# Modulation from free tiles, the sink as a score column, and a wider output projection in a two-layer hybrid attention kernel

## Chip, cores and metric

The kernel runs on one core of a Trainium2 chip. Times are device microseconds of one launch. The engines are named as in the profile: PE is TensorE, PEld its weight load, DVE VectorE, ACT ScalarE, POOL GpSimd, SP SyncE, which here only issues DMAs.

## What is computed

Two layers over 512 latent tokens and 256 context tokens of 1024 channels. Each layer normalises its tokens and modulates them by vectors from the conditioning (`w_mod`, 1024 x 3072 for each layer, gives shift, scale and gate), projects them by `w_in`, and feeds three attention branches: latent attention (MLA, 8 heads), differential attention (8 heads) and windowed attention with a sink logit for each of its 16 heads. Each branch's output is gated, projected by `w_branch`, weighted by a sigmoid gate and summed, and the sum goes through `w_out`:

```python
h_lat = rms_norm(x, norm_g) * (1.0 + scale) + shift
qc_l, kvc_l, kr_l, dq_l, dk_l, dv_l, sq_l, sk_l, sv_l, z_l, gm_l = split_cols(h_lat @ w_in)
...
p = jax.nn.softmax(jnp.concatenate([sk] + [s.astype(jnp.float32) for s in parts], axis=-1), axis=-1)
...
return (terms[0] + terms[1] + terms[2]) @ w_out
...
x = x + gate * merge_branches((ya_l, yb_l, yc_l), z_l, gm_l, w_branch, w_out)
```

`sk` is the sink: one logit for each head that takes part in the softmax and has no value behind it. The context tokens go the same way in the first layer; in the second only their keys and values are needed. The result is the latent stream after a final RMS norm with the weights `final_norm`.

## The kernel before, in words

All of it is one program whose order on every engine is written out beforehand by a planner. `Plan` keeps a simulated time and the time at which each engine is free (`P.on`, `P.pe`, `P.tick`, with costs such as `mm_cost` or the 550 ns of a modulation piece). Chains of instructions are Python generators that yield the time at which they are ready; `flush` emits the chain with the lowest rank first (`RANK`, line 42), and among equals the one that is ready first. Two streams feed PE: `stream_a` has the attention units (scores, transposes, values), `stream_b` the entries of a list (`plan_b`): the projections in the order of `SEQ`, then, for each branch, gates z and g and branch outputs b in the order of `BR`. An entry of `stream_b` starts when enough tiles are free (`need`, and `keep` more for the others), and the next one waits for it. What is emitted is fixed then; on the chip each engine works through its own list in order.

**Tiles and queues.** SBUF holds 46 large tiles of 128 x 768 (`slot`, `room`, `free`), nine of 128 x 512 (`pt`, taken by `tmps`), eight of 128 x 256 (`yo`). Weights come through `weight_stream`: a ring of two tiles `ws` (`NWS`) takes 512 KB at a time; each is split by ACT and DVE into a high and a low fp32r part in a ring of six tiles `wh` (`NWH`), since every product of the kernel is made of three fp32r passes (line 444 emits them). All DMAs are issued by SP (line 341).

**Modulation.** `mod_mm` (line 579) is a product with a stationary operand of 32 columns, written to the partitions 32g to 32g + 31 of a PSUM bank, g being the row block modulo 4. For the first layer's shift and scale this is done in the head (`mod_now`, eight products in a row). The other eight blocks of 512 columns (two for the gate of the first layer, six for the second) are done by `mod_entry`: four entries for each block, each with one tile `ws` of the weight ring and two products of 512 columns. They are put between the z, g and b entries of the first layer. `mod_fin` adds the four partial sums.

**Windowed attention.** `soft_sink` (line 849) works on a row of 128 queries of one head: a DVE instruction adds the mask and takes the maximum with the sink (858), another changes its sign (861), ACT takes the exponential of the sink alone and then of the row with its sum, DVE adds the two sums, takes the reciprocal (865), and `normalise` scales the row. There are 96 such rows in the first layer and 64 in the second.

**Output projection.** `out_entry` goes through four chunks of 256 columns, each for all tokens: for each half of the 1024 inputs and each token four steps of three passes into one PSUM bank. Each token's chain multiplies by the gate, adds the residual, squares with a sum, and after the last chunk normalises (`norm_rows` in the first layer; `rstd`, a scaling with `final_norm` and two stores in the second).

**Head.** `begin` loads modulation weights, x and the context tokens; `setup`, `setup1` and `setup2` load the small vectors (c, biases, norms, the lambda vectors of the differential attention, the sinks). `setup2`'s chain multiplies the lambda vectors on DVE.

## Time and profile before

| | us |
|---|---|
| median of 3 runs | 2752.4 |
| lowest and highest | 2744.74, 2753.49 |
| the profiled execution: its own time | 2746.83 |
| its span | 2745.0 |
| PE busy | 2657.7 |
| DVE, ACT, POOL busy | 1655.3, 1380.5, 127.8 |
| mean granted clock of PE | 0.988 |

The span is what the profile shows of one execution; the own time is a little longer. Times of rows are counted from the span's start. "busy" is the time in which an engine had an instruction at work; matmuls overlap, so the mean of one is longer than the step from one to the next, and that step is read from rows of equal matmuls in the timeline. What stands in brackets is idle time before an instruction and what ended it.

### The profile page before, as it was taken

To read this page: it belongs to the slowest core of one execution; us is meant where nothing else is said; L and a number is where in the kernel's file an instruction comes from. 1 tells how busy PE (TensorE), PEld (TensorE's weight loads), DVE (VectorE), ACT (ScalarE), POOL (GpSimd) and SP (SyncE) were. 2 spreads that over 40 slices of the span, in tenths; PEclk is the share of its full clock that TensorE was granted. 3 is DMA by queue.
4 is the path that set the end of the run, shared out by engine and by line. 5 is a ranking of instruction groups with operands and counts; after the bars stand their busy time and mean duration, and the time that the engine had idled before them with its cause. 6 is when DMAs were issued, how large, how long until landed. Compare 5 with 4: busy or idle time off the path is not lost.

```text
span 2745.0 us, 42932 instructions
## 1 busy us (share of the span) xinstructions
PE 2657.7 (97%) x16711; PEld 2308.7 (84%) x16711; DVE 1655.3 (60%) x3350; ACT 1380.5 (50%) x2860; POOL 127.8 (5%) x198
## 2 busy tenths in 40 slices
PE   7999999999999999999999999999999999999998
PEld 4888898888888878878888988898888789888888
DVE  4678778666676652133333578888767677634435
ACT  4667777555556442121222357877546555523332
POOL 0000000111100000000000000000011100000000
PEclk8999999999999999999999999999999999999999
DMA  6132211111122353353332443322112223443433
GB/s 228 45 92 83 73 42 46 49 51 48 44 68 87 107 187 105 93 175 93 91 86 62 139 125 92 105 57 67 40 48 55 58 68 102 127 136 110 123 101 130
DMA packets 328348, 249.58 MB, mean 91 GB/s; under 512 B 24548, under 2 KB 288320, under 8 KB 328144
## 3 DMA queue, kind: packets, MB, share of 16 engines
q1 hardware_dynamic: 328144, 246.83, 30.9%
q8 instruction: 131, 2.15, 0.3%
q14 instruction: 73, 0.60, 0.1%
HBM read 211.37 MB, written 35.41 MB: 90 GB/s over the span
## 4 chain that ended last, share of the span: by engine, by line
PE 78%; DVE 9%; ACT 7%; issue 3%; DMA 2%; POOL 1%; SPq 0%; DVEq 0%; ACTq 0%; POOLq 0%
PE wd L444 37%; PE bk L444 35%; PE bk L913 4%; ACT pt L309 3%; ACT s L309 3%; DVE pt L323 2%; DVE s L323 2%; PE bk L579 1%; DVE wh L323 1%; DVE s L858 1%; DVE s L330 1%; ACT wh L309 1%; DMA ws<-in_w_in_dram 1%; DVE ti L825 0%; POOL pt L325 0%
## 5 line engine op out<-in xcount | busy, mean ns | idle before, releaser
L444 PE MATMUL wd<-s,wh 128*128 128x512 f32 (+1 forms) x4392 | 855.5, 355 | 6.7 <-ACT wh L309 3.5
L444 PEld LDWEIGHTS wd<-s,wh 128*128 128x128 f32 x4392 | 725.7, 189 | 145.0 <-ACT s L309 12.9
L444 PE MATMUL bk<-s,wh 128*128 128x512 f32 (+1 forms) x3666 | 771.7, 356 | 18.4 <-DVE s L323 6.9
L444 PEld LDWEIGHTS bk<-s,wh 128*128 128x128 f32 x3666 | 582.5, 190 | 106.6 <-DVE s L323 9.8
L323 DVE TENSOR_TENSOR wh<-ws,wh 128x1024 fp32r<-128x1024 f32 (+4 forms) x294 | 325.1, 1112 | 343.1 <-ACT wh L309 341.4
L309 ACT ACTIVATE wh<-ws 128x1024 fp32r<-128x1024 f32 (+4 forms) x294 | 282.5, 967 | 297.1 <-PE wd L444 148.5
L309 ACT ACTIVATE pt<-bk 128x512 fp32r<-128x512 f32 (+3 forms) x604 | 341.4, 584 | 167.9 <-PE bk L913 102.8
L444 PE MATMUL bk<-wh,s 128*128 128x256 f32 x2688 | 352.9, 286 | 3.8 <-DVE wh L323 2.0
L444 PEld LDWEIGHTS bk<-wh,s 128*128 128x128 f32 x2688 | 333.3, 193 | 9.7 <-issue 3.2
L323 DVE TENSOR_TENSOR pt<-bk,pt 128x512 fp32r<-128x512 f32 (+3 forms) x400 | 257.6, 664 | 77.7 <-ACT pt L309 66.4
L444 PE MATMUL bk<-pt,s 128*128 128x256 f32 x1888 | 277.2, 288 | 13.3 <-DVE pt L323 10.2
L444 PEld LDWEIGHTS bk<-pt,s 128*128 128x128 f32 x1888 | 252.2, 191 | 38.8 <-DVE pt L323 16.7
L444 PE MATMUL wd<-s,s 128*128 128x256 f32 (+5 forms) x1872 | 275.9, 333 | 5.9 <-ACT s L309 5.5
L309 ACT ACTIVATE s<-wd,ti 128x768 f32<-128x768 f32 (+1 forms) x240 | 195.5, 818 | 140.8 <-DVE ti L825 78.5
L444 PEld LDWEIGHTS wd<-s,s 64*128 64x128 f32 (+2 forms) x1872 | 214.3, 191 | 36.7 <-ACT s L309 9.9
L913 PE MATMUL bk<-ident,s 128*128 128x128 f32 x1472 | 208.5, 275 | 9.8 <-DVE pt L323 2.4
L913 PEld LDWEIGHTS bk<-ident,s 128*128 128x128 f32 x1472 | 170.3, 142 | 35.9 <-ACT s L309 5.5
L309 ACT ACTIVATE s<-s,ti 128x512 f32<-128x512 f32 (+3 forms) x249 | 174.1, 708 | 15.0 <-DVE ti L865 8.1
L309 ACT ACTIVATE s<-bk 128x256 fp32r<-128x256 f32 (+5 forms) x291 | 113.6, 424 | 87.0 <-PE bk L444 85.0
L330 DVE SCALAR_TENSOR_TENSOR s<-s,wd 128x768 f32<-128x768 f32 (+1 forms) x58 | 47.6, 820 | 180.8 <-PE wd L444 108.1
L309 ACT ACTIVATE s<-wd 128x768 f32<-128x768 f32 (+1 forms) x58 | 40.9, 705 | 218.8 <-PE wd L444 218.8
L825 DVE TENSOR_REDUCE ti<-wd 128x1 f32<-128x768 f32 (+1 forms) x160 | 128.7, 843 | 18.2 <-PE wd L444 17.9
(98 smaller groups left out, 1734.6 us busy)
## 6 DMA issues: line engine op xcount, KB each, us to landing
ws<-in_w_in_dram SPq DMA_DIRECT2D x180, 512.0 KB
ws<-in_w_branch_dram SPq DMA_DIRECT2D x48, 512.0 KB
ws<-in_w_mod_dram SPq DMA_DIRECT2D x32, 512.0 KB
ws<-in_w_out_dram SPq DMA_DIRECT2D x24, 512.0 KB
y<-yo SPq DMA_DIRECT2D x80, 128.0 KB
s<-y SPq DMA_DIRECT2D x24, 384.0 KB
s<-s SPq DMA_DIRECT2D x22, 384.0 KB
s<-in_w_mod_dram SPq DMA_DIRECT2D x32, 256.0 KB
```

Source lines behind the costliest of these rows:

```text
L309: lambda: nc.scalar.activation(out=out, in_=in_, func=func, scale=scale, **kw))
L323: t = yield from dve(ready, lambda: nc.vector.tensor_tensor(out=out, in0=a, in1=b, op=op), n)
L330: t = yield from dve(ready, lambda: nc.vector.scalar_tensor_tensor(out=out, in0=a, scalar=s, in1=b, op0=op0, op1=op1), fsz(out), ptr=ptr)
L444: nc.tensor.matmul(o, lhsT=l, rhs=r, start=first, stop=last)
L579: nc.tensor.matmul(pm[32 * g:32 * g + 32, :], lhsT=sil[:, kt], rhs=wv, start=kt < 4, stop=kt >= 4)
L825: t = yield from dve(t, lambda: nc.vector.tensor_reduce(out=nmx, in_=p[:, lo:hi], axis=AX.X, op=ALU.max, negate=True), n)
L858: t = yield from dve(t, lambda: nc.vector.tensor_tensor_reduce(out=pt_[:, 0:n], in0=p[:, lo:hi], in1=mk, scale=1.0, scalar=sk, op0=ALU.add ...
L913: nc.tensor.transpose(out=pp[:, j * 256 + ri2 * 128:j * 256 + ri2 * 128 + 128], in_=row["P"][:, c:c + 128], identity=ident)
```

## The change

Six things. (1) A modulation piece takes 256 columns and all eight row blocks instead of 512 columns and two; its weights go in three DMAs to three free large tiles instead of the weight ring, and its products are a piece of their own for the planner (`P.pe`). (2) The scores and the mask of the windowed attention change their sign, the sink is copied by POOL as one more column behind the row, and one exponential with scale -1 covers row and sink with one sum. (3) The output projection takes 512 columns at a time, except that the second half of the latent tokens' columns is done in two steps of 256, the last one token by token; `final_norm` is multiplied in before the square sums are complete, and the last scaling is shared by ACT and DVE; the residuals are loaded before the gates. (4) The small vectors of `setup` and `setup1` are issued by ACT, those of `setup2` by POOL. (5) The values of the windowed attention are computed for the latent tokens first. (6) The weight splitter's rank goes from 2 to 1. The diff, cut to its core:

```diff
-RANK = (0, 1, 3, 0, 2)
+RANK = (0, 1, 3, 0, 1)
...
-    below = np.where(j >= i, 0.0, -1e30)
-    above = np.where(j <= i, 0.0, -1e30)
+    below = np.where(j >= i, 0.0, 1e30)
+    above = np.where(j <= i, 0.0, 1e30)
...
-    def dma(out, in_):
-        nc.sync.dma_start(out=out, in_=in_)
+    def dma(out, in_, eng=nc.sync):
+        eng.dma_start(out=out, in_=in_)
...
-        n, t = rows_of(sc, (c_in[0], c_ctx))
+        n, t = rows_of(sc, (c_in[0], c_ctx), nc.scalar)
...
-        dma(selt, sel)
+        dma(selt, sel, nc.scalar)
         st = slot()
-        n, t = rows_of(st, (b_mod[0], norm_g[0]))
+        n, t = rows_of(st, (b_mod[0], norm_g[0]), nc.scalar)
...
-        n, t = rows_of(st, (q_norm[0], kv_norm[0], subln[0], b_mod[1], norm_g[1], q_norm[1], kv_norm[1], subln[1]))
+        n, t = rows_of(st, (q_norm[0], kv_norm[0], subln[0], b_mod[1], norm_g[1], q_norm[1], kv_norm[1], subln[1]), nc.gpsimd)
         tv = 0.0
         for i, a in enumerate((lq1, lk1, lq2, lk2)):
-            tv = max(tv, dma(v[:, i * 128:(i + 1) * 128], a.rearrange("l d -> (l d)").partition_broadcast(128)))
-        dma(sinkt, sink.rearrange("l h -> (l h)").partition_broadcast(128))
+            tv = max(tv, dma(v[:, i * 128:(i + 1) * 128], a.rearrange("l d -> (l d)").partition_broadcast(128), nc.gpsimd))
+        ts = dma(sinkt, sink.rearrange("l h -> (l h)").partition_broadcast(128), nc.gpsimd)
         dma(rope, tab[:, 0:2 * LT].rearrange("p (a n) -> p a n", a=2))
 
         def chain():
+            yield from dve(ts, lambda: nc.vector.tensor_scalar(out=sinkt, in0=sinkt, scalar1=-1.0, scalar2=None, op0=ALU.mult), 32)
...
-    def mod_mm(pm, kt, wv):
+    def mod_mm(pm, kt, wv, c=0):
         g = kt % 4
-        nc.tensor.matmul(pm[32 * g:32 * g + 32, :], lhsT=sil[:, kt], rhs=wv, start=kt < 4, stop=kt >= 4)
+        nc.tensor.matmul(pm[32 * g:32 * g + 32, c:c + fsz(wv)], lhsT=sil[:, kt], rhs=wv, start=kt < 4, stop=kt >= 4)
...
-        mx, nmx, s, e, r = tiny(), tiny(), tiny(), tiny(), tiny()
-        sk = sinkt[:, u["l"] * 16 + row["h"]:u["l"] * 16 + row["h"] + 1]
+        nmx, s, r = tiny(), tiny(), tiny()
+        h = u["l"] * 16 + row["h"]
+        sk = sinkt[:, h:h + 1]
         yield room(1)
         pt_ = slot()
         row["P"] = pt_
         mk = u["mask"]()
+        yield from gps(0.0, lambda: nc.gpsimd.tensor_tensor(out=pt_[:, n:n + 1], in0=sk, in1=ones[:, 0:1], op=ALU.mult), 1)
         t = yield from dve(t, lambda: nc.vector.tensor_tensor_reduce(
-            out=pt_[:, 0:n], in0=p[:, lo:hi], in1=mk, scale=1.0, scalar=sk, op0=ALU.add, op1=ALU.max, accum_out=mx), n, ptr=True)
+            out=pt_[:, 0:n], in0=p[:, lo:hi], in1=mk, scale=1.0, scalar=sk, op0=ALU.add, op1=ALU.min, accum_out=nmx), n, ptr=True)
         rel.t = t
-        t = yield from dve(t, lambda: nc.vector.tensor_scalar(out=nmx, in0=mx, scalar1=-1.0, scalar2=None, op0=ALU.mult), 1)
-        t1 = yield from act(t, e, sk, func=AF.Exp, bias=nmx, psum=False)
-        t = yield from act(t1, pt_[:, 0:n], pt_[:, 0:n], func=AF.Exp, bias=nmx, accum=s, psum=False)
-        t = yield from tt(t, r, s, e, ALU.add)
-        t = yield from dve(t, lambda: nc.vector.reciprocal(out=r, in_=r), 8)
+        t = yield from act(t, pt_[:, 0:n + 1], pt_[:, 0:n + 1], func=AF.Exp, scale=-1.0, bias=nmx, accum=s, psum=False)
+        t = yield from dve(t, lambda: nc.vector.reciprocal(out=r, in_=s), 8)
...
-                for tp in range(3):
+                for tp in (1, 2, 0):
...
-                qk_entry("sq", pr, C_SQ, 0.125, cx)
+                qk_entry("sq", pr, C_SQ, -0.125, cx)
...
-        mod_left = [(n, j) for n in (2, 3, 0, 1, 4, 5) for j in range(4)]
+        mod_left = [(n, j) for n in (2, 3, 0, 1, 4, 5) for j in range(2)]
         pm = {}
 
         def mod_entry(ll, n, j):
-            it = item(lambda t: [(t[:, 0:1024].rearrange("p (k c) -> p k c", k=2),
-                                  w_mod[ll, j * 256:(j + 1) * 256, n * 512:(n + 1) * 512].rearrange("(k p) c -> p k c", p=128))], split=False)
-
-            def h(it):
-                yield lambda: max(at(it["ready"]), bk.gate() if j == 0 else 0.0)
-                if j == 0:
-                    pm["p"], pm["r"] = bk.take()
-                for k in range(2):
-                    mod_mm(pm["p"], 2 * j + k, it["ws"][:, k * 512:(k + 1) * 512])
-                P.tick(550.0)
-                if j == 3:
-                    P.spawn(mod_fin(ll, n, pm["p"], pm["r"], P.now + 200.0))
-            entry(h, [it], need=0)
+            def h():
+                W = [slot() for _ in range(3)]
+                t = 0.0
+                for i, w in enumerate(W):
+                    k = min(3, 8 - 3 * i)
+                    t = max(t, dma(w[:, 0:k * 256].rearrange("p (k c) -> p k c", k=k),
+                                   w_mod[ll, 384 * i:384 * i + 128 * k, n * 512 + j * 256:n * 512 + j * 256 + 256].rearrange("(k p) c -> p k c", p=128)))
+
+                def chain():
+                    def emit():
+                        if j == 0:
+                            pm[n] = bk.take()
+                        for k in range(8):
+                            mod_mm(pm[n][0], k, W[k // 3][:, k % 3 * 256:k % 3 * 256 + 256], 256 * j)
+                    te = yield from P.pe(lambda: max(t, bk.gate() if j == 0 else 0.0), 750.0, emit)
+                    free(3)
+                    if j == 1:
+                        yield from mod_fin(ll, n, *pm[n], te)
+                P.spawn(chain())
+                return
+                yield
+            entry(h, need=3, keep=KEEP_U)
...
+            def chain():
+                t = 0.0
+                for tk in toks:
+                    src = (x1_d[(tk - 2) * 128:(tk - 1) * 128] if l else x_in[0, (tk - 2) * 128:(tk - 1) * 128]) if tk >= 2 else ctx_in[0, tk * 128:(tk + 1) * 128]
+                    for h in range(2):
+                        t = max(t, dma(X[tk][h][:, 0:512], src[:, h * 512:(h + 1) * 512]))
+                G[j] = yield from tmps(2)
                 for h in range(2):
-                    t = max(t, dma(X[tk][h][:, 0:512], src[:, h * 512:(h + 1) * 512]))
-            o.rest[j] = t
-            if j == 0 and l == 1:
-                o.fn = yield from tmps(2)
-                for hh in range(2):
-                    dma(o.fn[hh][0], final_norm[hh * 512:(hh + 1) * 512].partition_broadcast(128))
-        o.rest = [0.0, 0.0]
-
-        def out_entry(toks, j, cchunk, last):
-            its = [item(wl_in(w_out[l], 256 * cchunk, k0=4 * i, kn=4, n=256)) for i in range(2)]
-
-            def o_h(i0, i1, c=cchunk):
+                    t = max(t, dma(G[j][h][0], gate_d[l][j, h * 512:(h + 1) * 512].partition_broadcast(128)))
+                if l == 1:
+                    o.fn = yield from tmps(2)
+                    for hh in range(2):
+                        t = max(t, dma(o.fn[hh][0], final_norm[hh * 512:(hh + 1) * 512].partition_broadcast(128)))
+                o.rest[j].t = t
...
+        def out_entry(toks, j, c, a0, n, last):
+
+            kn = 1024 // n
+            its = [item(wl_in(w_out[l], a0, k0=kn * i, kn=kn, n=n)) for i in range(8 // kn)]
+            final = a0 + n == 1024
+            steps = [(tk, k) for i in range(8 // kn) for tk in toks for k in range(kn * i, kn * i + kn)]
+            if final and j == 0:
+                steps = [(tk, k) for tk in toks for k in range(8)]
...
+                        (y, ry), = yield from tmps(1)
+                        y = y[:, 0:n]
+                        h, cc = a0 // 512, a0 % 512
+                        x = X[tk][h][:, cc:cc + n]
+                        yield o.rest[j]
+                        t = yield from tt(max(t, o.rest[j].t), y, o_["ps"][:, 0:n], G[j][h][0][:, cc:cc + n], ALU.mult)
                         o_["rel"].t = t
                         t = yield from tt(t, x, x, y, ALU.add)
-                        ry.t = t
-                        t = yield from square(t, x, s4[tk][:, c:c + 1])
-                        if c < 3:
+                        t2 = yield from act(t, y, x, func=AF.Square, accum=s4[tk][:, c:c + 1], psum=False)
+                        ry.t = t2
+                        if l == 1:
+                            t = yield from tt(t, x, x, o.fn[h][0][:, cc:cc + n], ALU.mult)
+                        if not final:
...
+                            t, r = yield from rstd(t2, s4[tk][:, 0:c + 1])
+                            xs = [X[tk][hh][:, 0:512] for hh in range(2)]
+                            ta = yield from act(t, xs[0], xs[0], scale=r, psum=False)
+                            t = yield from dve(t, lambda: nc.vector.tensor_scalar(out=xs[1], in0=xs[1], scalar1=r, scalar2=None, op0=ALU.mult), 512, fast=True, ptr=True)
+                            for hh, te in ((1, t), (0, ta)):
+                                yield from dmas(te, [(out[0, (tk - 2) * 128:(tk - 1) * 128, hh * 512:(hh + 1) * 512], xs[hh])])
...
-        for c in range(4):
-            out_entry(range(2, 6), 0, c, not cx)
+        wide_ = [(0, 512), (512, 512)]
+        for c, (a, n) in enumerate([(0, 512), (512, 256), (768, 256)]):
+            out_entry(range(2, 6), 0, c, a, n, not cx)
         if cx:
             entry(next_h, need=16)
-            for c in range(4):
-                out_entry(range(2), 1, c, True)
+            for c, (a, n) in enumerate(wide_):
+                out_entry(range(2), 1, c, a, n, True)
 
 
     xs0, xd0 = {}, {}
```

## Rows read from the trace of the kernel before

**Rows 1.** The page, busy us of each engine (share of the span), instructions.
```profile
PE 2657.7 (97%) x16711; PEld 2308.7 (84%) x16711; DVE 1655.3 (60%) x3350; ACT 1380.5 (50%) x2860; POOL 127.8 (5%) x198
```

**Rows 2.** Windows: stretch, length, busy us (count) by engine, granted PE clock, DMA share, GB/s.
```profile
36.00:60.00 24.00, 16.42 (x66) 12.24 (x66) 14.47 (x39) 14.86 (x39) 2.68 (x2) 0.72 0.53 169
98.00:480.00 382.00, 366.39 (x2453) 330.30 (x2452) 302.68 (x862) 282.12 (x678) 18.04 (x17) 0.98 0.23 63
940.00:1262.00 322.00, 313.58 (x1756) 248.61 (x1755) 114.09 (x150) 87.83 (x130) 0.00 (x0) 0.99 0.45 139
1660.00:1912.00 252.00, 242.63 (x1529) 214.71 (x1528) 216.37 (x572) 196.75 (x436) 14.18 (x11) 1.00 0.30 79
```

**Rows 3.** Timeline of PE, modulation products: start, us, instruction, count (merged).
```profile
33.06 1.99 PE L579 MATMUL bk<-s,sil 128*32 128x512 f32 x14
...
1061.77 1.05 PE L579 MATMUL bk<-ws,sil 128*32 128x512 f32 x4
1062.75 8.62 PE L444 MATMUL wd<-s,wh 128*128 128x512 f32 x48
```

**Rows 4.** Groups by form, modulation pieces: count, busy us, mean ns, idle before.
```profile
L579 PE MATMUL bk<-ws,sil 128*32 128x512 f32 x128 | 31.5, 614 | 1.6 <-DMA ws<-in_w_mod_dram 1.6
```

**Rows 5.** Waits of PE from 940 to 1262 us: us in total, times, longest.
```profile
PE wd L444 <- ACT wh L309: 3.5, 3, 1.6
PE wd L444 <- DVE wh L323: 2.5, 3, 1.5
PE bk L579 <- DMA ws<-in_w_mod_dram: 1.6, 1, 1.6
```

**Rows 6.** Timeline, wide matmuls of the last branch and second layer's output projection.
```profile
2589.67 99.44 PE L444 MATMUL wd<-s,wh 128*128 128x512 f32 x438
...
2688.95 46.23 PE L444 MATMUL bk<-wh,s 128*128 128x256 f32 x384
```

**Rows 7.** Timeline of the tail.
```profile
2734.96 6.97 SPq L341 DMA_DIRECT2D out_dram<-s  x8
...
2738.25 1.07 POOL L657 TENSOR_TENSOR ti<-ti,mhalf 128x1 f32<-128x1 f32 x2 [2.50 <-DVE ti L655]
2738.84 2.74 DVE L330 SCALAR_TENSOR_TENSOR s<-s,ti,pt 128x512 f32<-128x512 f32 x4 [0.47 <-POOL ti L657]
```

**Rows 8.** Groups by form, one-column instructions of the sink softmax, and POOL's.
```profile
L309 ACT ACTIVATE ti<-sinkt,ti 128x1 f32<-128x1 f32 x160 | 42.8, 289 | 16.6 <-DVE ti L861 16.0
...
L325 POOL TENSOR_TENSOR pt<-pt,rope 128x512 f32<-128x512 f32 x52 | 67.1, 1290 | 764.3 <-ACT pt L309 595.5 <-PE bk L444 52.0 <-DVE ti L861 46.8
...
L323 DVE TENSOR_TENSOR ti<-ti,ti 128x1 f32<-128x1 f32 x160 | 24.6, 157 | 23.3 <-ACT s L309 22.1
...
L861 DVE TENSOR_SCALAR ti<-ti 128x1 f32<-128x1 f32 x160 | 21.6, 142 | 0.3
...
L657 POOL TENSOR_TENSOR ti<-ti,mhalf 128x1 f32<-128x1 f32 x16 | 10.9, 683 | 1355.0 <-DVE ti L656 1352.4 <-DVE ti L655 2.5
L979 POOL TENSOR_TENSOR ti<-ti 128x2 f32<-128x2 f32 x40 | 8.8, 220 | 32.5 <-DVE ti L840 32.4
```

**Rows 9.** Timeline of the head, SP's issues, POOL and PE.
```profile
5.26 0.43 SPq L341 DMA_DIRECT2D selt<-in_sel_dram  x1
...
7.86 1.03 SPq L341 DMA_DIRECT2D s<-in_x_dram  x2
...
33.78 0.35 SPq L341 DMA_DIRECT2D s<-in_mla_q_norm_dram  x1
...
42.70 0.43 SPq L341 DMA_DIRECT2D sinkt<-in_swa_sink_dram  x1
...
48.70 2.13 POOL L657 TENSOR_TENSOR ti<-ti,mhalf 128x1 f32<-128x1 f32 x1 [6.00 <-DVE ti L656]
...
49.27 1.65 PE L444 MATMUL bk<-s,wh 128*128 128x512 f32 x3 [3.76 <-DVE s L323]
```

**Rows 10.** Waits of VectorE from 36 to 60 us.
```profile
DVE s L323 <- DMA s<-in_diff_lk_dram: 4.3, 2, 2.5
```

52 lines of the change are left out of this document (23 added, 29 removed).

## The prediction

> **What bounds the kernel now.** The page first: TensorE (PE) is busy 2657.7 us of a span of 2745.0 [rows 1]. Busy is not the same as at full rate, so the windows by stage come next [rows 2]: they show where PE is idle or granted less than full clock. The idle time is small and lies in few places: 24.0 - 16.4 = 7.6 us in the head's second part (36 to 60 us, granted clock 0.72), 382.0 - 366.4 = 15.6 us in the first layer's windowed attention (clock 0.98, that is 7.6 us more at the lower of its two levels, 1.2 for 2.4 GHz), 322.0 - 313.6 = 8.4 us where the modulation is computed, 252.0 - 242.6 = 9.4 us in the second layer's windowed attention. So there are two ways to gain: give PE less to do, which counts in full almost anywhere, or fill these holes, which counts up to their size. Then the list of groups by form, for the prices of what goes, and the timeline, for how fast PE takes a row of equal matmuls.
>
> The profiled execution took 2746.8 us (span 2745.0 and 1.8 around it); the median of the runs shown, 2752.4, lies 5.6 above it. The sum is made against 2746.8. About 0.3% (8 us) is what a measurement of this kernel can tell from no change.
>
> **Modulation.** Before, a piece is two products of 512 columns, which occupy two of the four 32-column groups of the array. From the start of one piece to the wide matmul behind it: 1062.75 - 1061.77 = 0.98 us [rows 3]. 32 pieces give 31.5 us, as the group's busy time says too [rows 4]. After, a piece is eight products of 256 columns over all four groups. How they share the array is seen in the head, where eight products of 512 columns in the same four groups took 1.99 us [rows 3]: as long as two pieces, not four. Half the columns make about 1.0 us. There are 16 such pieces: 16 us, against 31.5. I take **-15.5**. The bounds: nothing, if the short products don't overlap (16 pieces at 1.97); -19, if they scale without the start-up. I stay by the nearest row, the 1.99.
>
> The pieces also leave the weight stream's ring of two tiles. In 940 to 1262 us PE waits 3.5 + 2.5 us for the split of weights and 1.6 us for a piece's own load [rows 5], 7.6 in all, since a load of 512 KB for a piece stands between two loads of weights. After, 48 issues (three of up to 384 KB for each piece) replace 32 on SP's queue, each waits for a free tile, and weights queue behind them; but the DMA engines are at a share of 0.45 there [rows 2]. I take **-5**; bounds -8.4 and +5 (a megabyte ahead of a weight load takes some 3.4 us at 139 GB/s for a share of 0.45, that is 309 GB/s; a few such waits).
>
> **Output projection.** 438 matmuls of 512 columns took 99.44 us, 0.227 each; 384 of 256 took 46.23, 0.1204 each [rows 6]. One wide for two narrow saves 0.0138. For the latent tokens the first half of the columns goes wide in both layers (96 wide for 192 narrow, twice), for the context tokens of the first layer everything (96 for 192): 288 x 0.0138 = **-4.0**, all of it PE work. VectorE's multiplication by final_norm moves ahead of the last step; it lies under the matmuls of the next token, which take 24 x 0.120 = 2.9 us for the last quarter.
>
> **Tail.** The last matmul ends at 2688.95 + 46.23 = 2735.2, the span at 2745.0: 9.8 us. Four tokens arrive together there: POOL's last two powers stand until 2739.3, four scalings follow until 2741.6, the eight stores' issue ends at 2741.9, and 3.1 us pass to the end [rows 7]. Token by token, only one is left: about 0.3 to start, 2.1 for multiply, add and square, 1.3 for mean and power, 0.7 for the scaling (now split between ScalarE and VectorE), 0.4 to issue, 3.1 to land: 7.9 at most, some 7.3 with the two engines side by side. **-2.5**; bounds 0 and -4.
>
> **Sink as a column.** Each of 160 rows loses one ScalarE exponential of one column (289 ns), an addition (157) and a sign change (142) on VectorE, and gains a copy on POOL; its nearest rows are POOL's two-column products at 220 ns [rows 8]. In the first layer's 96 rows that is 28 us of ScalarE's 282 and 29 of VectorE's 303 [rows 2, 8], at engines that run at three quarters. None of it is on PE itself; what can come back is PE's idle time and lost clock there, 15.6 + 7.6 + 9.4 = 33 us. A tenth less work on both engines fills a third of it, by my choice: **-10**. The bounds are 0 (PE then waits for other chains) and -33. The changed order of V's tokens and the splitter's rank go with this: they shift the same holes.
>
> **Small vectors.** In the head VectorE stood 4.3 us waiting for the diff_lk vectors [rows 10], with the splits of h behind it in order, and PE then waited 3.76 us for these splits [rows 9]. The vectors came late as SP issued 13 of them from 33.78 to 43.1 [rows 9]. At the start x's loads begin at 7.86, after three small issues that begin at 5.26 [rows 9]: 2.6 us in a stage whose DMA engines are the limit soon after. I take 4.3 + 2.6 = **-7**, rounded. ScalarE gets five issues ahead of its first tanh; at SP's 0.43 us for one [rows 9] that is about 2 us, and the first products wait for their weights anyway. No transfer issued by POOL is in this trace: nearest are SP's 0.43 us [rows 9] and, for what POOL can suffer beside VectorE, a power that took 2.13 us [rows 9] for 0.68 in the mean [rows 8]. By the first POOL is done in 13 x 0.43 = 5.6 us, by the second in 27.7. Bounds: -14 (the part's 7.6 idle and its clock loss of 6.7) and +14 (the second). I stay by the first, the commoner.
>
> **Sum:** 15.5 + 5 + 4 + 2.5 + 10 + 7 = 44: 2746.8 - 44 = 2703. The four executions of before reach from 2744.7 to 2753.5, with their middle 2.8 above the profiled one; I add 2: **2705**.
>
> **The rivals.**
> *Only PE's own work counts* (0.21): the holes move and stay as large. -15.5 - 4 - 2.5 = -22: 2725. For it: PE's order is written out in advance, and a hole's releaser is often the next chain in line. Against it: two of the holes have named causes that go.
> *The holes close* (0.12): sink -24 and head -14 and ring -8.4: -68, 2679.
> *POOL's transfers are slow* (0.09): the head loses 14 instead of 7 gained: 2726. POOL's power beside VectorE's two-input subtractions took three times its usual [rows 8, 9]. The Trainium skill ("SBUF - State Buffer", the section on its two separate sides) says that a DMA from POOL's queue has its descriptors written by POOL and starves while VectorE holds the port that they share, and that ScalarE's or SP's queue would not; by that rule this part is the wrong way round. The 2.13 us row agrees that the two block each other, though it is no transfer.
> *The free tiles aren't free* (0.07): a piece needs three tiles with two to spare, and the stream of weights stops where they are missing. The first four pieces come while MLA still holds tiles, around 945 to 975; PE loses at most the 8 us of fill that they were: 2713.
> *Slower* (0.06): the copy on POOL comes too late. POOL works in order, and a rope multiplication of 1.29 us, 52 of them [rows 8], that waits for ScalarE holds the copies behind it, for which the exponential waits. If a third of 1.29 us, 0.43, falls on PE's path for each of 160 rows, that is +69 in place of -10: 2784. It decides from 0.28 us a row ((2746.8 - 2703) / 160). Against it: POOL is busy 18 of 382 us there [rows 2], and the copy can start with the row's mask step, which takes longer.
> No change (0.03) is left for mixtures of these. The forecast has 0.42.
>
> **The numbers.** The range takes in the forecast, the rivals 2725, 2726 and 2713 and, at its edge, 2679: 2679 to 2733; slower, no change and the far part of the larger gain are left out. Faster: 0.42 + 0.21 + 0.12 + 0.09 + 0.07 = 0.91.
>
> **What would show it.** Right: 16 modulation pieces of about 1.0 us and some 16 us of busy time; no wait for wh among them; 46 us of output projection down to about 45; some 7 us from last matmul to end; VectorE without its wait for diff_lk and PE full before 55 us; ScalarE and VectorE each some 28 us less in the first windowed attention. Wrong: pieces of 1.9 us; POOL's issues of 2 us each with VectorE waiting behind them; exponentials released by POOL; new waits of PE of more than 10 us in any stage.

## The result and the profile after

The changed kernel takes 2710.9 us (median of four executions, 2709.7 to 2714.0), the kernel before beside it 2750.6: a ratio of 0.986, 95% interval 0.9841 to 0.9879. The forecast was 2705 with a range of 2679 to 2733. The profiled execution of after took 2711.5 us (span 2709.7), 35.3 less than that of before. One of the 12 executions of "Projection and rank on the kernel before", further down, took 2932.0 us at a mean granted clock of 0.841 and is left out of that run's median and ratio.

Part of the gain goes along with PE's granted clock. The kernel before was run 65 times beside the experiments; its mean granted clock lies between 0.981 and 0.991, and its time falls with it, from 2756.9 us at 0.981 to 2740.8 at 0.991. A straight line through the 65 gives some 1.8 us for each 0.001 (an estimate). Beside after, before has 0.986 in the mean and after 0.991, so some 9 of the 39.7 us between the medians go along with the clock. How much of that the edits earned isn't shown.

The page of after, busy us of each engine (share of the span) and instructions, against [rows 1]:

```profile
PE 2632.3 (97%) x16551; PEld 2291.5 (85%) x16551; DVE 1615.4 (60%) x3010; ACT 1350.7 (50%) x2685; POOL 179.3 (7%) x371
```

PE lost 25.4 us of busy time, VectorE 39.9, ScalarE 29.8; POOL gained 51.5. To see where the 35.3 us came from, both spans are cut at the same milestones: the first sink row, the last differential row of layer 1, the first product of the wide branch, its last, the first transposition of layer 2, its first sink row, its last differential row, the end. Windows of before, cut there (stretch, length, busy us (count) of PE, PEld, DVE, ACT and POOL, granted PE clock, DMA share, GB/s):

```profile
0.00:98.80 98.80, 80.11 (x455) 59.00 (x456) 45.15 (x118) 49.04 (x124) 8.18 (x14) 0.90 0.55 180
98.80:798.20 699.40, 676.61 (x4656) 599.17 (x4656) 523.37 (x1292) 459.54 (x1069) 58.05 (x93) 0.99 0.21 56
...
798.20:975.70 177.50, 172.10 (x1177) 150.59 (x1175) 117.04 (x223) 101.42 (x234) 1.94 (x5) 0.99 0.34 103
975.70:1534.70 559.00, 553.03 (x3125) 466.80 (x3124) 185.31 (x214) 130.87 (x162) 0.00 (x0) 1.00 0.36 109
1534.70:1588.80 54.10, 54.10 (x453) 54.10 (x452) 30.60 (x62) 19.03 (x43) 1.95 (x3) 1.00 0.58 191
1588.80:1656.30 67.50, 62.22 (x433) 57.19 (x432) 45.97 (x88) 39.60 (x83) 4.34 (x5) 1.00 0.38 107
1656.30:2213.30 557.00, 543.10 (x3628) 475.63 (x3628) 430.93 (x944) 374.67 (x794) 49.12 (x69) 0.99 0.24 63
2213.30:2745.00 531.70, 516.40 (x2798) 446.23 (x2796) 276.91 (x415) 206.29 (x355) 4.23 (x9) 0.99 0.39 114
```

Windows of after, the same columns and milestones:

```profile
0.00:92.50 92.50, 77.74 (x455) 56.97 (x456) 44.76 (x119) 48.79 (x124) 16.32 (x29) 0.93 0.60 192
92.50:790.60 698.10, 680.44 (x4710) 605.04 (x4710) 507.07 (x1106) 443.02 (x975) 81.50 (x187) 0.99 0.21 58
...
790.60:930.20 139.60, 133.97 (x950) 123.35 (x950) 96.28 (x186) 85.09 (x197) 2.24 (x5) 1.00 0.30 87
930.20:1494.80 564.60, 563.63 (x3425) 484.65 (x3424) 199.27 (x245) 145.00 (x197) 0.00 (x0) 1.00 0.39 117
1494.80:1545.20 50.40, 50.40 (x315) 45.66 (x314) 27.95 (x51) 16.86 (x34) 1.66 (x3) 1.00 0.53 178
1545.20:1611.50 66.30, 62.60 (x382) 55.88 (x381) 44.62 (x81) 42.12 (x80) 4.24 (x5) 1.00 0.42 120
1611.50:2181.80 570.30, 549.79 (x3641) 480.57 (x3640) 421.86 (x821) 363.97 (x736) 69.14 (x134) 0.99 0.24 64
```

The differences of the lengths: head -6.3; attention of layer 1 -1.3; the two stretches of MLA and the wide branch, with the modulation in them, 736.5 to 704.2, that is -32.3; layer 1's output projection -3.7; the start of layer 2 -1.2; attention of layer 2 **+13.3**; the rest (527.9 of 531.7) -3.8. The sum is -35.3. The planner writes a new order for each kernel, so the stretches don't hold quite the same matmuls (the counts show it, 4710 for 4656 in the second); idle time, length less busy, is the safer reading. In layer 1's attention it fell from 22.8 to 17.7 us, in layer 2's it rose from 13.9 to 20.5. The clock is in these lengths too. PE's busy time at the lower of its two clock levels (1.2 for 2.4 GHz), added up from the two traces, rose in layer 2's attention from 5.1 to 13.7 us, which is some 4 of its +13.3; in the head it fell from 14.5 to 11.0, some 1.8 of its -6.3, beside 4.0 us less idle.

The steps that the prediction named are these rows. Groups by form of after (modulation pieces; the exponential with the sink as its last column; POOL's copy), for [rows 4] and [rows 8]:

```profile
L580 PE MATMUL bk<-s,sil 128*32 128x256 f32 x256 | 18.0, 385 | 0.7 <-DMA s<-in_w_mod_dram 0.4
...
L309 ACT ACTIVATE s<-s,ti 128x513 f32<-128x513 f32 x64 | 45.8, 718 | 9.1 <-DVE ti L862 7.5 <-POOL s L861 1.5
...
L861 POOL TENSOR_TENSOR s<-sinkt,ones 128x1 f32<-128x1 f32 x160 | 43.9, 308 | 68.2 <-PE bk L914 37.6 <-DMA q<-s 7.2 <-ACT s L309 7.1
```

Timeline of after, PE around a piece, for [rows 3]:

```profile
1105.73 1.07 PE L580 MATMUL bk<-s,sil 128*32 128x256 f32 x16
1106.73 7.88 PE L444 MATMUL wd<-s,wh 128*128 128x256 f32 x42
```

A piece (sixteen records for its eight products) takes 1.00 us to the next matmul, and the 16 pieces 18.0 us of busy time for 31.5. In all 160 rows ScalarE waits for POOL's copy once, for the 1.5 us shown: what the slower rival needed, 0.28 us a row, isn't there. Of the signs that the prediction named, one came out smaller: in the stretch of after that matches the first windowed attention of [rows 2] VectorE has 22.6 us less to do and ScalarE 20.7, for some 28 (the two stretches don't hold quite the same matmuls).

### The profile page after: what moved, and what is told of

Its sections match the earlier page's. It is cut to its first block, busy times and chain, and to the rows that moved or that the text cites. A ratio compares the mean times of both kernels' runs of the same rounds, so it can differ in the third digit from the quotient of the medians.

```text
span 2709.7 us, 42486 instructions
## 1 busy us (share of the span) xinstructions
PE 2632.3 (97%) x16551; PEld 2291.5 (85%) x16551; DVE 1615.4 (60%) x3010; ACT 1350.7 (50%) x2685; POOL 179.3 (7%) x371
## 5 line engine op out<-in xcount | busy, mean ns | idle before, releaser
L444 PE MATMUL wd<-s,wh 128*128 128x512 f32 (+1 forms) x4392 | 852.2, 355 | 2.0 <-DVE s L330 1.5
L444 PEld LDWEIGHTS wd<-s,wh 128*128 128x128 f32 x4392 | 723.7, 189 | 123.1 <-issue 6.7
L444 PE MATMUL bk<-s,wh 128*128 128x512 f32 (+1 forms) x3666 | 763.4, 355 | 8.0 <-DVE s L323 1.8
L444 PEld LDWEIGHTS bk<-s,wh 128*128 128x128 f32 x3666 | 584.2, 190 | 94.9 <-issue 6.8
L444 PE MATMUL bk<-wh,s 128*128 128x256 f32 (+1 forms) x2400 | 351.3, 300 | 3.9 <-DVE pt L323 3.0
L444 PEld LDWEIGHTS bk<-wh,s 128*128 128x128 f32 x2400 | 319.0, 192 | 19.8 <-DVE pt L323 3.7
L323 DVE TENSOR_TENSOR pt<-bk,pt 128x512 fp32r<-128x512 f32 (+5 forms) x428 | 273.3, 656 | 89.7 <-ACT pt L309 69.8
L444 PE MATMUL bk<-pt,s 128*128 128x256 f32 x1888 | 282.7, 289 | 16.2 <-DVE pt L323 10.6
L444 PEld LDWEIGHTS bk<-pt,s 128*128 128x128 f32 x1888 | 252.5, 192 | 41.0 <-DVE pt L323 19.4
L444 PE MATMUL wd<-s,s 128*128 128x256 f32 (+5 forms) x1872 | 274.3, 332 | 10.2 <-ACT s L309 7.4
L444 PEld LDWEIGHTS wd<-s,s 64*128 64x128 f32 (+2 forms) x1872 | 210.3, 190 | 38.8 <-ACT s L309 11.9
L309 ACT ACTIVATE s<-s,ti 128x513 f32<-128x513 f32 (+6 forms) x256 | 183.1, 722 | 26.6 <-DVE ti L862 11.0
L309 ACT ACTIVATE yo<-bk 128x256 f32<-128x256 f32 (+1 forms) x200 | 72.2, 382 | 141.3 <-PE bk L444 140.1
L862 DVE CUSTOM_DVE_ANT_0 s<-wd,s,sinkt 128x512 f32<-128x512 f32 (+2 forms) x160 | 116.3, 743 | 42.1 <-PE wd L444 41.9
```

What stands on the lines that cost most here:

```text
L309: lambda: nc.scalar.activation(out=out, in_=in_, func=func, scale=scale, **kw))
L323: t = yield from dve(ready, lambda: nc.vector.tensor_tensor(out=out, in0=a, in1=b, op=op), n)
L444: nc.tensor.matmul(o, lhsT=l, rhs=r, start=first, stop=last)
L862: t = yield from dve(t, lambda: nc.vector.tensor_tensor_reduce(out=pt_[:, 0:n], in0=p[:, lo:hi], in1=mk, scale=1.0, scalar=sk, op0=ALU.add ...
```

## The experiments

The changed kernel is made of five edits: modulation, output projection, sink, queues of the small vectors, and order (V's tokens and the splitter's rank). Each run is timed against the kernel before on the same chip; ratios are to it. After is 0.986 by this scale.

**Modulation alone.** The pieces from free tiles in 256 columns, all else as before.

```diff
-        mod_left = [(n, j) for n in (2, 3, 0, 1, 4, 5) for j in range(4)]
+        mod_left = [(n, j) for n in (2, 3, 0, 1, 4, 5) for j in range(2)]
...
+                W = [slot() for _ in range(3)]
...
+                        for k in range(8):
+                            mod_mm(pm[n][0], k, W[k // 3][:, k % 3 * 256:k % 3 * 256 + 256], 256 * j)
```

> The kernel before with the modulation part alone (free tiles, pieces of eight products of 256 columns). My theory: 16 pieces of about 1.1 us, as in the changed kernel (18.0 us of busy time for 31.5), and the waits of PE for the weights' split between 940 and 1262 us gone: 18 to 22 us less, a ratio of 0.992 to 0.993. Rival, only PE's own work counts: 13 to 14 us less, 0.995. Rival, the order written by the planner shifts and gives part of it back elsewhere: under 10 us less.

Measured: 2718.8 us, ratio 0.9898 [0.9873, 0.9922]; some 28 us, more than expected. The waits of PE for the weight stream during the modulation are gone; in 940 to 1262 us, where [rows 5] had 7.6 us, one is left:

```profile
PE wd L444 <- DVE s L330: 0.3, 1, 0.3
```

Windows of before and of this run, from the last differential row to the last wide product of layer 1:

```profile
798.20:1535.00 736.80, 725.43 (x4302) 617.70 (x4301) 302.35 (x436) 232.33 (x396) 1.94 (x5) 1.00 0.36 107
```

```profile
795.30:1504.60 709.30, 705.80 (x4430) 616.66 (x4430) 298.91 (x432) 233.74 (x399) 1.94 (x5) 1.00 0.37 112
```

The stretch is 27.5 us shorter, and 11.4 us of idle became 3.5. So the ring's share is about 8 us of idle. The other 19.6 are busy time of PE: most of it the pieces', and some 3 us the clock, since before spends 6.3 us of this stretch at the lower level and this run none.

**Output projection alone.** 512 columns, last quarter token by token.

```diff
-        for c in range(4):
-            out_entry(range(2, 6), 0, c, not cx)
+        for c, (a, n) in enumerate([(0, 512), (512, 256), (768, 256)]):
+            out_entry(range(2, 6), 0, c, a, n, not cx)
```

> The kernel before with the output projection alone (512 columns, last quarter token by token). My theory after seeing the changed kernel: 4 us less PE work, and nothing in the tail, since the tokens' chains stand behind each other on VectorE: 9.5 us from PE's last matmul to the end, as in the changed kernel, for 9.8 before. About 4 us less in all, 0.9985. Rival as predicted blind: the tail falls to 7.3 us, 6.5 us less in all.

Measured: 2755.1 us, ratio 1.0023 [1.0012, 1.0033]: slower by 6 us. The waits of PE around the output projection of layer 1 and the start of layer 2 (1535 to 1667 us): us in total, times, longest:

```profile
PE bk L444 <- DVE wh L323: 7.1, 2, 5.3
...
PE bk L444 <- ACT wh L309: 1.3, 1, 1.3
```

In before the first of these is 2.0 us. The splits of the wide weights come late: ScalarE and VectorE have other chains in front of them. Behind such a wait PE also goes on at the lower clock. Its next matmuls, and the whole stretch:

```profile
1587.54 5.91 PE L444 MATMUL bk<-wh,s 128*128 128x512 f32 x13 [1.78 <-DVE wh L323]
```

```profile
1535.00:1667.00 132.00, 120.98 (x701) 106.54 (x701) 75.70 (x135) 56.44 (x110) 6.01 (x8) 0.95 0.42 133
```

Thirteen wide matmuls take 0.45 us each, for 0.227 at full clock [rows 6]; the granted clock of the stretch is 0.95, for 1.00 in before's two. It is 9 us longer than there: 5.7 us of idle and some 6.5 of clock (an estimate from the time at the lower level), less 3 of PE work. The tail is 9.5 us, as the expectation had it.

**Small vectors alone.** ScalarE's and POOL's queues for the vectors, SP's for the rest.

```diff
-        n, t = rows_of(sc, (c_in[0], c_ctx))
+        n, t = rows_of(sc, (c_in[0], c_ctx), nc.scalar)
...
-            tv = max(tv, dma(v[:, i * 128:(i + 1) * 128], a.rearrange("l d -> (l d)").partition_broadcast(128)))
+            tv = max(tv, dma(v[:, i * 128:(i + 1) * 128], a.rearrange("l d -> (l d)").partition_broadcast(128), nc.gpsimd))
```

> The kernel before with the small vectors alone on ScalarE's and POOL's queues. My theory: PE's first sink row's mask step starts some 6 us earlier than the 98.8 us of before, and the time is 6 us less, 0.998. Rival: the gain at the head comes from the order of V's tokens, which is not in this kernel, and the first row starts less than 3 us earlier.

Measured: 2745.0 us, ratio 0.9987 [0.9972, 1.0003]. The first sink row comes at 95.9 us for 98.8, 2.9 us earlier, so the rival of less than 3 came out. The interval of the total holds no change as well as such a gain, and the mean granted clock of this run (0.988 for before's 0.986) would by itself be some 4 us of it.

**Sink alone.** The column, with SP still loading the vector.

```diff
+            yield from dve(ts, lambda: nc.vector.tensor_scalar(out=sinkt, in0=sinkt, scalar1=-1.0, scalar2=None, op0=ALU.mult), 32)
...
-        t1 = yield from act(t, e, sk, func=AF.Exp, bias=nmx, psum=False)
-        t = yield from act(t1, pt_[:, 0:n], pt_[:, 0:n], func=AF.Exp, bias=nmx, accum=s, psum=False)
-        t = yield from tt(t, r, s, e, ALU.add)
+        t = yield from act(t, pt_[:, 0:n + 1], pt_[:, 0:n + 1], func=AF.Exp, scale=-1.0, bias=nmx, accum=s, psum=False)
```

> The kernel before with the sink as a column alone. Predicted blind: 10 us less, 0.996. Theory after seeing the changed kernel, in which the second layer took 9 us more from its first transposes to the last matmul (1155.0 for 1146.4): the sink's column gains some 7 us in the first layer's windowed attention and loses as much in the second layer, where the exponential waits for POOL's copy: no change, 0.998 to 1.002, with the second layer at 1150 to 1156. Rival: the second layer's loss has nothing to do with the sink, and the second layer stays at 1142 to 1147 here.

Measured: 2746.7 us, ratio 0.9996 [0.9984, 1.0008]: nothing. Part of the reason stands in the head. Waits of VectorE from 30 to 62 us:

```profile
DVE sinkt L556 <- DMA sinkt<-in_swa_sink_dram: 5.8, 1, 5.8
```

The sign change of the sink vector is new in the head, and it stands in front of the splits of h and waits for the last of SP's 13 small loads; in before, VectorE waited 4.3 us there for the one ahead of it [rows 10] and nobody needed the sinks until the first row. The first sink row comes 1.3 us later, though the null change below has that too (1.4); the wait itself is new. The second layer, from its first transposition to its last matmul, takes 1154.0 us for before's 1146.4, which says nothing of the sink: the small vectors alone show 1151.4 and the null change 1151.1. Then the attention of layer 1 shows 22.5 us idle for 22.8, though VectorE and ScalarE have less to do:

```profile
100.10:792.10 692.00, 669.53 (x4656) 594.33 (x4655) 506.83 (x1108) 435.20 (x964) 79.48 (x187) 0.99 0.21 57
```

The four ratios multiply to 0.9904; the whole is at 0.986, a difference just clear of the intervals taken together. Either the parts need one another, or the fifth edit, the order, does it, which none of the four has. The next runs ask.

**After without the new rank.** One number of the splitter.

```diff
-RANK = (0, 1, 3, 0, 1)
+RANK = (0, 1, 3, 0, 2)
```

> The changed kernel with one number put back: the splitter's last rank 2 again in place of 1, so that the splits of the weight stream queue behind more of the chains. Theory (the wide output projection pays only with that rank, because its weights' splits come late at the junction of the layers without it): 5 to 12 us above the changed kernel's 2710.9, that is 0.988 to 0.990 of before, and PE waits again for wh at L444 and in the output projection between 1490 and 1620 us, some 8 to 11 us idle there. Rival (the rank is nothing by itself, the loss seen with the output projection alone was an unlucky plan): within 3 us of 2710.9, ratio 0.985 to 0.987.

Measured: 2715.8 us, ratio 0.9877 [0.9856, 0.9897]. The interval overlaps with that of after, so the 5 us alone decide nothing; the waits do. From 1499 to 1622 us, the same stretch as above:

```profile
PE bk L444 <- DVE wh L323: 7.0, 2, 5.4
```

This wait is the 7.1 us of the projection alone. In after, the same part has no wait for wh at all; one wait of 3.7 us for the normalised rows is left:

```profile
PE wd L682 <- DVE s L665: 3.7, 1, 3.7
```

From the first product of the projection to layer 2's first sink row that is 122.2 us for after's 116.4, of which 3.5 is idle time and some 2 the clock (0.97 for 1.00). The attention of layer 1:

```profile
93.40:790.60 697.20, 674.78 (x4656) 600.16 (x4655) 506.00 (x1106) 437.41 (x966) 78.38 (x187) 0.98 0.21 57
```

Here 22.4 us are idle, for after's 17.7. Yet up to the last matmul PE is idle for 68.1 us in this run and for 67.9 in after: over the whole kernel the rank moves the holes and doesn't fill them.

**Projection and rank on the kernel before.** The diffs of the two together.

> The kernel before with the new output projection and the new rank, nothing else. Alone, the projection gave 2755.1 (1.0023 of before). Theory (with the rank it pays its 4 us of PE work and the waits of PE for wh at the junction of the layers go): 2740 to 2746, ratio 0.9965 to 0.9985. Rival (the rank isn't it, or the plan of before has no place for it): 2752 to 2760, ratio 1.001 to 1.0035, with PE again 8 us or more idle between 1530 and 1670 us.

Measured: 2758.2 us, ratio 1.0025 [1.0013, 1.0037]: no better than the projection alone. The waits for wh are gone, as the theory had it, but in their place stand 5.3 us for the normalised rows, and the attention of layer 1 now shows 27.4 us idle. The biggest wait in it is about that of before (8.7 us for 8.9); new are waits for scaled rows (L802) and for the maximum of the old sink's rows (L858):

```profile
99.50:806.80 707.30, 679.86 (x4691) 601.41 (x4690) 529.32 (x1300) 456.35 (x1061) 57.58 (x93) 0.99 0.21 57
```

```profile
PE bk L913 <- DVE s L802: 2.6, 2, 2.3
PE wd L444 <- DVE ti L858: 2.4, 1, 2.4
```

The theory held at the place that it named and fell in the total.

**After without the sink as a column.** The diff of the sink, taken back.

> The changed kernel with the old sink (the one-column exponential, the addition and the sign change on ScalarE and VectorE, no copy on POOL, the old sign of the masks), all else as changed. Theory of the prediction: 10 us are lost, 2721, ratio 0.9895 to 0.990. Theory after the run of the sink alone (the column is worth nothing that can be measured, since PE's waits in these stages are for other chains in line): 2708 to 2714, ratio 0.9845 to 0.9875. In both, ScalarE and VectorE show some 28 us more busy time in the first layer's windowed attention.

Measured: 2725.0 us, ratio 0.9911 [0.9894, 0.9928], clear of after's interval: 14 us slower, where the sink alone gave nothing. The theory built on that run fell; the 10 us of the prediction are nearer. Layer 1's attention:

```profile
92.60:797.70 705.10, 679.26 (x4691) 600.90 (x4690) 529.01 (x1299) 456.38 (x1061) 57.58 (x93) 0.99 0.21 57
```

25.8 us idle for after's 17.7, with as many instructions in it as in the run before this one (4691 matmuls, 1061 of ScalarE). Over the whole of the two profiled executions 8 us are idle time (75.9 for 67.9) and 5 busy time, about what the clock accounts for: 56.7 us at the lower level for 45.2, a mean of 0.988 for 0.991. So 8 us are shown to be waits that the column ends.

**A null change.** The same instructions on the same data; a constant of the planner shifts the order.

```diff
-TOPE = 125.0
+TOPE = 130.0
```

> The kernel before with one constant of the planner at 130 in place of 125: the same instructions on the same data, in another order. It prices what any re-planning does by itself. Theory (the planner's luck is worth several us, and so several parts of the change under 8 us can't be told from it): a time that differs from before by 3 to 10 us either way, in other holes than before. Rival (the plan is robust): within 3 us of 2749.9, ratio 0.999 to 1.001.

Measured: 2748.4 us, ratio 0.9998 [0.9985, 1.0012]. One such shift moved the median by less than 2 us, so the rival is nearer for it. The profiled executions were less steady in detail: layer 2's attention took 563.6 us in this one for 557.0, from the first sink row to the last differential one. Some 4 of these 6.6 us are the clock (13.4 us at the lower level for 5.1), and 2.2 are idle time (16.1 for 13.9).

**Sink and rank on the kernel before.** The two diffs together.

> The kernel before with the sink as a column and the splitter's rank 1, nothing else. Idle time of PE from the first sink row to the last differential row in layer 1, by the four runs so far: old sink and rank 2 22.8 us, column and rank 2 22.5, old sink and rank 1 27.4 (seen with the new projection), both new 17.7 (the changed kernel). Theory (the two belong together: the column gives VectorE room and the rank decides that the chains which PE waits for get it): 17 to 19 us idle there, 2740 to 2744 in all, ratio 0.996 to 0.998. Rival (the 17.7 come from the rest of the change, such as V's token order): 22 us or more idle there, ratio 0.999 to 1.002.

Measured: 2747.0 us, ratio 1.0001 [0.9992, 1.001]. Head and attention of layer 1:

```profile
0.00:102.40 102.40, 80.59 (x454) 58.50 (x455) 45.11 (x118) 48.79 (x124) 9.03 (x16) 0.87 0.53 174
102.40:793.90 691.50, 674.84 (x4691) 599.83 (x4690) 504.91 (x1102) 441.37 (x970) 81.42 (x187) 0.99 0.21 58
```

Idle in the attention: 691.5 - 674.8 = 16.7 us, as the theory wanted (17 to 19), and not the rival's 22. The total gained nothing all the same: the head is 3.6 us longer, VectorE standing 6.1 us for the sink vector, and the attention of layer 2 has 19.7 us idle for 13.9 in before. Up to the last matmul PE is idle for 78.2 us, for 77.5 in before. Both halves of the expectation came out by themselves, and they don't add as either theory had it.

So layer 1's attention is a table of two by two (idle us of the profiled executions): old sink and old rank 22.6 to 23.1 (before and four runs on it); column alone 22.5 (on before) and 22.4 (in after); new rank alone 27.4 (with the projection) and 25.8 (in after); both 16.7 to 19.0 (this run, after and three runs on it). In this stage the column pays with the rank and not without it.

**After without the new output projection.** The old projection and tail, all else as changed.

> The changed kernel with the old output projection (256 columns throughout, the old order in the last quarter, VectorE's old tail). Theory of the prediction: PE's 4 us and the tail's are lost, 2714 to 2717, ratio 0.987 to 0.988. Theory after the runs of the projection alone (it pays at the last projection, but its late weights and longer chains cost 5 to 8 us where the layers meet and in the second layer): 2703 to 2707, ratio 0.983 to 0.9845, faster than the changed kernel.

Measured: 2712.3 us, ratio 0.9874 [0.9855, 0.9893], 1.5 us above after by the medians and 3.8 by the ratios, since the kernel before was faster on this chip: within the intervals, and against the theory that the projection costs 5 us here. Its last projection takes 46.23 us as in before [rows 6], that of after 44.95:

```profile
2655.27 44.95 PE L444 MATMUL bk<-wh,s 128*128 128x512 f32 x288
```

That of layer 1 takes 54.1 for 50.4; the start of layer 2 takes 64.0 for 66.3 and gives 2.3 us back. Its first sink row comes at 94.1, for 92.5 in after, although this edit changes nothing in the head: so much is scatter between orders. The projection is worth between nothing and 4 us; with the late weights cured by the rank it does no harm.

**Both scalings of the tail on ScalarE.**

```diff
-                            t = yield from dve(t, lambda: nc.vector.tensor_scalar(out=xs[1], in0=xs[1], scalar1=r, scalar2=None, op0=ALU.mult), 512, fast=True, ptr=True)
-                            for hh, te in ((1, t), (0, ta)):
+                            t = yield from act(ta, xs[1], xs[1], scale=r, psum=False)
+                            for hh, te in ((0, ta), (1, t)):
```

> The changed kernel with both scalings of a finished token on ScalarE, so that VectorE has no instruction that waits for POOL's power. Theory (the last token's product starts 2.2 us after its matmuls end since VectorE, in order, stands 0.7 us a token in front of the scaling): VectorE's next product starts within 0.6 us of the last matmul, and from the last matmul to the end of the span 7.8 to 8.4 us in place of 9.5, though the second scaling on ScalarE adds 0.72; in the time 1 to 2 us, which is less than can be measured. Rival (the chain through ScalarE's square and POOL's power is the length itself): 9.5 to 10.2 us.

Measured: 2710.9 us, ratio 0.9871 [0.9853, 0.989]; from the last matmul's end (2703.15) to the end of the span (2712.5) 9.35 us, for after's 9.5. The theory fell: VectorE no longer waits for POOL, but it waits for ScalarE, whose two scalings stand in front of the next token's square. VectorE's multiplications by final_norm, which follow the square, and ScalarE's scalings:

```profile
2703.28 0.42 DVE L323 TENSOR_TENSOR s<-s,pt 128x256 f32<-128x256 f32 x1 [1.65 <-ACT pt L309]
...
2704.69 1.33 ACT L309 ACTIVATE s<-s,ti 128x512 f32<-128x512 f32 x2 [1.44 <-POOL ti L658]
2705.93 0.40 ACT L309 ACTIVATE pt<-s 128x256 f32<-128x256 f32 x1
...
2706.45 0.43 DVE L323 TENSOR_TENSOR s<-s,pt 128x256 f32<-128x256 f32 x1 [1.70 <-ACT pt L309]
```

A token takes 3.2 us this way as well (2706.45 - 2703.28), more than the 2.9 us of its matmuls. The last token's first product does start sooner, 0.7 us after the last matmul for 2.2 in after; its square then waits.

**The same, with ScalarE's vectors back on SP's queue.**

> As the run before it, and the vectors that ScalarE's queue loads (c, the selection, b_mod, norm_g) back on SP's queue. Theory (ScalarE's issues of up to 1.7 us each hold its first tanh, 7.07 us against 3.20 before, and PE's first product of the main work starts 2 us later for it): the first product of a row of 512 columns at L444 at 36.7 to 37.3 in place of 38.8, the first sink row 1 to 2 us earlier, 2706 to 2709 in all. Rival (x's loads wait on SP behind these again and the head is bound by the transfers): no earlier first sink row than 92.5, 2710 to 2713.

Measured: 2716.7 us, ratio 0.989 [0.9873, 0.9908]: no faster, and by the medians 5.8 us above the run before it, of which the head explains 1.4 and the clock up to 3 (0.990 for 0.9915 in the mean). Timeline of its start (SP's and PE's):

```profile
4.40 5.25 PE L580 MATMUL bk<-s,sil 128*32 128x512 f32 x9 [1.49 <-DMA s<-in_w_mod_dram]
...
7.71 1.13 SPq L341 DMA_DIRECT2D s<-in_x_dram  x2
```

and that of after:

```profile
6.03 3.13 SPq L341 DMA_DIRECT2D s<-in_x_dram  x5
...
7.83 1.94 PE L580 MATMUL bk<-s,sil 128*32 128x512 f32 x8 [3.18 <-DVE sil L527]
```

PE's first product comes 3.4 us earlier and is worth nothing, since it waits for the weights; x's loads come 1.7 us later, and the first sink row 1.4 (93.8 for 92.4). The first product of a row of 512 columns, which the theory wanted at 36.7 to 37.3, comes at 40.31, later than the 38.8 that it was to beat; ScalarE's issues, which it put at up to 1.7 us each, take 0.28 to 0.59 in after. The rival had the head (no first sink row before 92.5), though its 2710 to 2713 for the total was missed too. So it pays here to keep these vectors off SP's queue. No run beat the changed kernel.

## Why the prediction was right

The direction, the range and the largest term held. By the medians the total missed by 6 us; by the two profiled executions, against which the sum was made, by 9 (35.3 for 44). That the medians come nearer is luck in part, since they set a before of 0.986 granted clock against an after of 0.991.

The 44 were 19.5 us of PE's own work (modulation and projection), 22 of waits (ring, sink, vectors) and 2.5 of tail. The two profiles show 25.4 us less busy time, 9.6 us less idle time up to the last matmul (2735.2 - 2657.7 = 77.5 before, 2700.2 - 2632.3 = 67.9 after) and 0.3 in the tail. Of the busy time 13.5 are the pieces, about 4 the projection and some 2 the clock; no run tells where the other 6 went. So work gave more than forecast, and waits less than half: those that ended were partly replaced by others, above all in layer 2.

**Modulation: right.** -15.5 was forecast, -13.5 measured (18.0 us of busy time for 31.5, pieces of 1.00 us). The four groups of the array share 256-column products as the head's 512-column ones had shown [rows 3]. The forecast's 32 pieces at 0.98 us left out that six of before's stand in pairs, and that a pair can take no longer than one piece:

```profile
944.79 1.07 PE L579 MATMUL bk<-ws,sil 128*32 128x512 f32 x8
```

The next instruction starts at 945.79, 1.00 us later; the pair at 962.73 takes 1.00 as well, the one at 968.62 takes 1.39. So before had some 29 us of steps for 16 after, 13 by steps.

**Waits for the ring: right in kind, too small.** -5 was taken from bounds of -8.4 and +5; alone, the edit removed 8 us of idle, and in that run all of [rows 5] but 0.3 us is gone. In after the two stretches have 4.8 us less idle than in before (6.6 for 11.4), and 3.5 with the old rank: the new rank takes 3 back. Alone the choice inside the bounds was too careful: the loads that the change adds on SP's queue found room at a DMA share of 0.4.

**Output projection: the PE work is right, its setting was missed.** The last projection fell from 46.23 to 44.95 us, 1.3, just 96 x 0.0138. But the step "all of it PE work" left out who makes the weights: in wider pieces, with the old rank, their splits came up to 5.3 us late, PE went on at the lower clock after that, and the edit alone was slower by 6 us. The prediction set the rank down as a part of the sink. It serves the projection too: with it the 7 us of waits for wh are absent, shown by two runs that differ in it alone.

**Tail: wrong.** -2.5 was forecast, 9.5 us for 9.8 measured. The failed step is "only one is left". The tokens do finish one by one, but each needs VectorE, ScalarE and POOL in turn, three queues in order, and a token's round takes longer than its 2.9 us of matmuls. Timeline of after:

```profile
2700.59 0.42 DVE L323 TENSOR_TENSOR s<-s,pt 128x256 f32<-128x256 f32 x1 [0.57 <-ACT pt L309]
...
2701.99 0.49 DVE L1856 TENSOR_SCALAR s<-s,ti 128x512 f32<-128x512 f32 x1 [0.73 <-POOL ti L658]
2702.39 0.42 DVE L323 TENSOR_TENSOR pt<-bk,pt 128x256 f32<-128x256 f32 x1
...
2705.31 0.72 ACT L309 ACTIVATE s<-s,ti 128x512 f32<-128x512 f32 x1 [1.44 <-POOL ti L658]
```

The last matmul ends at 2700.2, yet the last token's first product starts at 2702.39, behind the token before it: 2.2 us, nearly the whole of the forecast gain. The prediction gave the last token 0.3 us to start. An order in which a token's first product and square go ahead of the scalings of the one before might be the remedy; it wasn't tried.

**Sink: near in size within the change, by luck in part, and wrong in its reason.** The forecast was -10 by filling a third of 33 us of holes; taken out of after, the column costs 14 us (8 of them idle time, most of the rest clock), in the kernel before it gives none, and column and rank together give none there either. The work did go: VectorE's and ScalarE's busy time fell by 39.9 and 29.8 us over the kernel. But less work on an engine fills a hole only if the chain that PE waits for is the one that moves up, and this the rank decides in layer 1 (the table of two by two), and the vector's own load decides in the head. The prediction looked for the copy's risk on POOL and found none; the sign change, one instruction of 0.18 us in the head, was a DMA wait of 5.8 us when SP loaded the vector last. On POOL's queue it is harmless. In layer 2 the holes did not close: 13.9 us of idle became 20.5, and this goes with the rank: every run with the old one has 12.7 to 16.1 there, every run with the new 17.2 to 20.5. In the three pairs of runs that differ in it alone, the old rank and the new show 13.7 and 20.5 (after), 14.3 and 18.4 (projection), 14.8 and 19.7 (sink). So the rank gives 5 us in layer 1 with the column, 7 us of waits for the wide weights, and takes 4 to 7 in layer 2 and 3 in the wide branch. Which chain it holds up there stays open, and a rank for each layer wasn't tried.

**Small vectors: right in the head's sum, which is not the vectors' alone.** -7 forecast, the head is 6.3 us shorter. VectorE's wait for diff_lk is gone, PE's 3.76 us for the splits shrank to single waits of 0.8, x's loads begin at 6.03 for 7.86. The vectors alone gave 2.9; the sink and the rank don't shift the first row within after (92.6 and 93.4 without them), the modulation alone didn't either (99.0), and some 1.8 us are the clock. The rest may be V's changed order of tokens, which wasn't run alone; as first sink rows scatter by 1 to 2 us between orders (94.1 without the projection, 100.2 after the null change), it isn't shown.

**The rivals.** POOL's transfers were not slow. Timeline of after, POOL and VectorE:

```profile
20.36 0.88 DVE L665 TENSOR_SCALAR s<-s,ti 128x512 f32<-128x512 f32 x2 [0.66 <-POOL ti L658]
20.37 0.96 POOL L341 DMA_DIRECT2D s<-in_mla_q_norm_dram  x1
21.33 0.53 POOL L341 DMA_DIRECT2D s<-in_mla_kv_norm_dram  x1
...
27.10 1.62 DVE L703 TENSOR_SCALAR pt<-wd,modc 128x512 f32<-128x512 f32 x2
...
27.32 0.54 POOL L341 DMA_DIRECT2D s<-in_diff_lq_dram  x1
...
28.39 0.54 POOL L341 DMA_DIRECT2D sinkt<-in_swa_sink_dram  x1
```

Twelve of the 13 issues took 0.51 to 0.59 us, and all are out from 20.37 to 28.9, before the head's crowded stretch: 8.6 us, for the 5.6 that the prediction took from SP's issues. The first took 0.96, about as long as the two scalings from SBUF to SBUF that VectorE ran beside it (0.88 for both). By the Trainium skill ("SBUF — State Buffer", the section on its two separate sides) that is what a lock on the shared port would look like; the trace agrees with it in this one issue, at 0.4 us. But the first issue took 0.95 to 0.97 in all seven kernels here that load by POOL, and each time it was both the queue's first and beside those scalings, so a cost of the first issue isn't ruled out. VectorE's scalings out of PSUM, at 27.10, held none. No issue in these runs stood beside much work of VectorE, so what the rival feared was hardly put to the test. *Free tiles not free*: no wait of PE for a piece's tiles was seen from 988 us to the end of the wide branch. *Only PE's own work* (2725): nearer than its time says, since 25.4 of the 35.3 us are busy time; the holes did move, into layer 2, but the ring's, the head's and layer 1's are worth more. *Slower*: refuted by the 1.5 us above. The times of two rivals leave out the 2 us that the forecast adds (2727 and 2681 with them), which changes nothing.

## What to carry to other kernels

Work taken off an engine that isn't the bound pays only through a wait that it ends: look which chain the bottleneck waits for and whether the schedule (here a rank) lets that chain use the room. Before judging an edit, ask which other edit it leans on: here the column leaned on the rank in layer 1, the wide projection on the rank, and alone each of them measured nothing or a loss. That the column also leaned on the moved load is argued from its wait in the head; a run of column, rank and moved load without the rest wasn't made. And when work is cut to finish item by item, compare the round trip of one item through all its in-order engines with the time between items; if it is longer, the tail stays. Before a difference of a few us is put down to an edit, compare the granted clocks of the two runs: here 0.005 between two means stands for some 9 us.
